# Hybrid attention, convolution and state-space layer: attention of all head pairs as one pipeline of block steps, decay matrices prepared in pairs

## The chip, the cores and the metric

The kernel runs on one core of a Trainium2 chip. The metric is device microseconds of one launch. A core has engines with instruction streams of their own: TensorE (PE in the profile; its weight loads are PEld), VectorE (DVE), ScalarE (ACT), GpSimd (POOL) and SyncE (SP), which here issues most of the loads. They meet only through semaphores. TensorE's matmuls and transposes write into PSUM; ACT and DVE empty it. Each engine takes its instructions strictly in the order in which they stand in its stream.

## The reference

One layer of a hybrid backbone over 128 context tokens and 256 latent tokens (384 together), model width 2048. Cut to what matters here:

```python
hcur = x * (1 + sc1) + sh1                     # modulation 1
q, k, v, u, gt, z, xbc, dt = split(hcur @ w_in)
o_a = attention(q, k, v)                       # 16 heads of 64: context rows dense,
                                               # latent rows over a window plus cached context keys
o_b = silu(layer_norm(dwconv31(u * sigmoid(gt))))
y   = ssd_scan(x, dt, a, B, C, h0)             # both directions, chunks of 128 tokens
      # decay matrix seg = exp(cs_i - cs_j); scores = (C B^T) * seg; y_diag = scores @ (x dt)
o_c = rms_norm((y_f + y_b + d_skip * xs) * silu(z))
mix = concat(o_a, o_b, o_c) @ w_out
x   = layer_norm(ALPHA * x + g1 * mix)
hcur = x * (1 + sc2) + sh2                     # modulation 2
x   = layer_norm(ALPHA * x + g2 * conv_ffn(hcur))
```

All of it is float32 with outputs for both token groups, the context keys and values, and the final states.

## The kernel before

The 384 tokens are three blocks of 128: block 0 is the context, blocks 1 and 2 the latents. A product with a large weight is taken as three fp32r matmuls: weight and activation are split into a high part (a cast on ACT, `whi`, `hl`) and a remainder (a subtraction on DVE, `wlo`, `hl`), and high by high, high by low and low by high are summed in PSUM. These triples (lines 454 to 456 and 460 to 462) are called the main matmuls here.

Up to 275 us the kernel takes modulation 1 and the first part of the input projection; from 590 us on the rest of the output projection, a layer norm and the feed-forward part. The change lies in the stretch between, 275 to 590 us. There a main stream runs: the projections for z and dt, for v, then eight pairs of key and query tiles (one per pair of heads), then the first column group of the output projection (`wo_group(0)`), whose sixteen row blocks come in `ORDER`: the convolution's four (8 to 11), attention 0 to 3, the state space's four (12 to 15), attention 4 to 7. `cat_split` casts and subtracts a row block before it is used. The order of PE's instructions in this stretch is exactly the order in which the program issues them; the other engines' streams are arranged by a scheduler from priorities.

Between the main matmuls stand steps of side work, which are Python generators. The class `_Flow` keeps a clock of assumed PE time: each `flow.tick(us)` of the main stream moves it on, and generators whose due time has come run one step. A step ends with `yield cost, delay`: its assumed PE time and how long until its next step is due. The generators are `tok_gen` (transposes of the state-space inputs), `ssm_gen` (which calls `chunk_steps` for each of three chunks of tokens and adds "ssm" to the set `ready` at its end), `conv_ln_gen` (the layer norm of the convolution), `attn_gen`, `mod2_gen` (part of modulation 2 on PE, lines 768 to 801, whose raw weights lie in the three `v` buffers) and `sh2_gen`, which begins when "ssm" is ready and sums one shift of modulation 2 on DVE (line 832).

- `attn_gen` handles one head pair: `scores` of block 0; then three times `turned` of a block (six transposes of the probabilities into PSUM tiles `at`, copied out by ACT, lines 723 and 725) with `scores` of the next block behind it (lines 695 to 713: PE, then a maximum on DVE, exponential on ACT, reciprocal on DVE, scaling on ACT into `p`, three buffers); then `values` (line 736, into one more `at` tile, copied out by ACT at line 739). There are two `at` tiles in all. From head pair 5 on, a pair begins only when "ssm" is ready.
- `chunk_steps` makes for each of two head groups the decay matrix W (`decays`: DMA and mask on POOL, exponentials on ACT, products on DVE), waits 15 us of flow time, and multiplies (lines 576 to 582).
- `conv_ln_gen` normalises four channel blocks in place in `cvo` and ends with SiLU (line 397) into four new `t` buffers, which become row blocks 8 to 11.
- `mod2_end` adds the bias and either writes the gate by four small DMAs on POOL's queue (group 0) or transposes the scales (group 1). Its two work tiles are `gb` buffers, of which there are three, which also carry the attention's bias tables.

Of the kernel before, what the change touches and what calls it, by code (L numbers as in the profile page):

```python
# [99 lines left out]
def _build(tc, ctx, a):  # L100
# [39 lines left out]
    def gb_t():  # L140
        return sbt([128, 640], "gb", 3)
# [223 lines left out]
    def conv_ln_gen():  # L365
        while flow.bg:
            yield 0.0, 1.0
        yield 0.0, 3.0
        n = 399
        ps = at_t()  # L370
        for i in range(4):
            PE.matmul(ps[:, :n], ones, cvo[i][:, :n], start=i == 0, stop=i == 3)
        mu = g_t()
        S.activation(out=mu[:, :n], in_=ps[:, :n], func=AF.Copy, scale=1.0 / 512)
        yield 2.7, 3.0
        sqs = []
        for i in range(4):
            V.tensor_tensor(out=cvo[i][:, :n], in0=cvo[i][:, :n], in1=mu[:, :n], op=ALU.subtract)
            sq = g_t()
            S.activation(out=sq[:, :n], in_=cvo[i][:, :n], func=AF.Square)  # L380
            sqs.append(sq)
            yield 0.0, 2.0
        sm = at_t()
        for i in range(4):
            PE.matmul(sm[:, :n], ones, sqs[i][:, :n], start=i == 0, stop=i == 3)
        rs = g_t()
        S.activation(out=rs[:, :n], in_=sm[:, :n], func=AF.Sqrt, scale=1.0 / 512, bias=eps_t)
        yield 2.7, 0.0
        for c0, c1 in ((0, 133), (133, 266), (266, 399)):
            yield 0.0, 3.0  # L390
            V.reciprocal(out=rs[:, c0:c1], in_=rs[:, c0:c1])
        for i in range(4):
            yield 0.0, 2.0
            V.tensor_tensor(out=cvo[i][:, :n], in0=cvo[i][:, :n], in1=rs[:, :n], op=ALU.mult)
        for i in range(4):
            c = t_t(T)
            for (c0, c1, o0) in ((0, PT, 0), (PT, T, 143)):
                S.activation(out=c[:, c0:c1], in_=cvo[i][:, o0:o0 + c1 - c0], func=AF.Silu,
                             scale=P_("cln_g", i), bias=P_("cln_b", i))
            cat[8 + i] = c  # L400
            ready.add(8 + i)

    xact = [None] * 8
    xtok = [None] * 3
# [164 lines left out]
    def chunk_steps(c):  # L569
        y = m_t()  # L570
        V.tensor_tensor(out=hv(y), in0=hv(xtok[c]), in1=bc(P_("d_skip", 0, 8), 2, 64), op=ALU.mult)
        for g in range(2):
            W = decays(c, g)
            yield 0.0, 15.0
            psg = at_t()
            PE.matmul(psg[:, :128], xact[4 + g][:, OFF[c]:OFF[c] + 128], xact[6 + g][:, OFF[c]:OFF[c] + 128])
            V.tensor_tensor(out=W, in0=W, in1=bc(psg[:, :128], 1, 4), op=ALU.mult)
# [163 lines left out]
    qk = {}  # L741

    def attn_gen():
        for hp in range(8):
            while hp not in qk or (hp >= 5 and "ssm" not in ready):
                yield 0.0, 0.5
            q, k = qk[hp]
            bias = [gb_t() for _ in range(2)]
            for e in range(2):
                G.dma_start(out=bias[e], in_=a["bias"][2 * hp + e])  # L750
            p = scores(hp, q, k, 0, bias)
            yield 0.65, 5.5
            pts = []
            for blk in range(3):
                pts.append(turned(blk, p))
                if blk < 2:
                    p = scores(hp, q, k, blk + 1, bias)
                yield (1.25, 1.8, 0.75)[blk], (6.0, 6.0, 2.5)[blk]
            values(hp, pts)
            ready.add(hp)  # L760
            yield 2.0, 0.0

    gS = {}

# [16 lines left out]

    def mod2_end(g):
        ps = gS.pop(g)
        sm = gb_t()[:, :512]
        if g == 0:
            bg = gb_t()[:, :512]
            pinned(bg, a["bgate"])
            with tc.high_priority(offset=HP):
                V.tensor_tensor(out=sm, in0=ps, in1=bg, op=ALU.add)
# [175 lines left out]
    def cat_split(k):  # L965
# [6 lines left out]
        ta, tb = cg0[k // 4]  # L972
        ch[k], cl[k] = ta[:, k % 4, :], tb[:, k % 4, :]
        with tc.high_priority(offset=HP):
            split(cat[k], ch[k], cl[k])

    cg0 = [None] * 4
    with tc.manual_schedule(engines={mybir.EngineType.PE}):
# [360 lines left out]
```

## Time and profile before

| quantity | value |
|---|---|
| median of three runs | 1825.29 us (1822.78 to 1829.71) |
| the profiled execution's own time | 1823.79 us |
| its span, first to last instruction | 1822.0 us |
| mean granted TensorE clock | 0.995 |
| PE busy | 1784.0 us (98%) |
| DVE busy | 1216.2 us (67%) |
| ACT busy | 780.6 us (43%) |
| POOL busy | 64.2 us (4%) |

The 1.8 us between span and time lie outside the first and last instruction. A timeline row gives the start of an instruction, its duration and, in brackets, the time its engine was idle before it and what ended that. Matmuls overlap, so what one costs the stream is read from the distance between starts: the main matmuls stand 0.23 us apart and last 0.39 us each.

### The profile page before, as it was taken

How to read it: one execution, taken by the hardware profiler on the slowest of the kernel's cores; microseconds unless marked ns; L12 is line 12 of the kernel's file. 1: busy time of each engine (PE TensorE's matmuls, PEld its weight loads, DVE VectorE, ACT ScalarE, POOL GpSimd, SP SyncE). 2: the span in 40 equal slices, each digit the busy share in tenths (PEclk: the TensorE clock that was granted, in tenths of full speed). 3: DMA queues.
4: the chain of work that ended last, by engine and by line, in shares of the span. 5: the costliest groups of instructions: out<-in, count | busy, mean ns of one | idle time of the engine just before them, and what ended most of it. 6: DMA issues, size and time to landing. Idle time of an engine off the chain costs nothing. (4 is left out here: it accounts for less than half of the span.)

```text
span 1822.0 us, 28856 instructions
## 1 busy us (share of the span) xinstructions
PE 1784.0 (98%) x10794; PEld 1621.9 (89%) x10794; DVE 1216.2 (67%) x2587; ACT 780.6 (43%) x1467; POOL 64.2 (4%) x149
## 2 busy tenths in 40 slices
PE   7999999989998999999999999999999999999998
PEld 6888997878886899999989999988999988999987
DVE  3866899775599977667534676545666544766577
ACT  4223454556664336444333444323444423444424
POOL 0000001011002000000000000000000000000000
PEclk9999999999998999999999999999999999999999
DMA  8899467656798852444544454444544444445454
GB/s 314 312 317 323 142 202 253 234 191 217 242 337 303 268 176 64 147 141 145 155 125 137 162 174 145 150 127 133 174 159 152 151 124 143 158 149 157 122 150 139
DMA packets 113260, 337.76 MB, mean 185 GB/s; under 512 B 13096, under 2 KB 17672, under 8 KB 113120
## 3 DMA queue, kind: packets, MB, share of 16 engines
q1 hardware_dynamic: 105888, 311.65, 52.2%
q0 software_dynamic: 7232, 24.28, 4.3%
q8 instruction: 84, 1.38, 0.3%
q14 instruction: 56, 0.46, 0.1%
HBM read 331.08 MB, written 4.79 MB: 184 GB/s over the span
## 5 line engine op out<-in xcount | busy, mean ns | idle before, releaser
L229 ACT CAST whi<-raw 128x512 fp32r<-128x512 f32 (+1 forms) x755 | 467.8, 621 | 878.0 <-PE mm L461 289.5
L230 DVE TENSOR_TENSOR wlo<-raw,whi 128x512 fp32r<-128x512 f32 (+1 forms) x755 | 519.1, 689 | 409.9 <-ACT whi L229 405.0
L460 PE MATMUL mm<-hl,whi 128*128 128x384 f32 x1245 | 426.4, 342 | 1.5 <-ACT whi L229 1.2
L461 PE MATMUL mm<-hl,whi 128*128 128x384 f32 x1245 | 419.9, 337 | 0.0
L462 PE MATMUL mm<-hl,wlo 128*128 128x384 f32 x1245 | 419.2, 337 | 0.0
L460 PEld LDWEIGHTS mm<-hl,whi 128*128 128x128 f32 x1245 | 233.8, 188 | 11.7 <-issue 4.9
L461 PEld LDWEIGHTS mm<-hl,whi 128*128 128x128 f32 x1245 | 234.0, 188 | 1.1 <-DVE wlo L230 0.4
L462 PEld LDWEIGHTS mm<-hl,wlo 128*128 128x128 f32 x1245 | 233.9, 188 | 0.0
L460 PE MATMUL sc<-hl,whi 128*128 128x384 f32 x659 | 222.9, 338 | 0.0
L461 PE MATMUL sc<-hl,whi 128*128 128x384 f32 x659 | 221.9, 337 | 0.0
L462 PE MATMUL sc<-hl,wlo 128*128 128x384 f32 x659 | 221.8, 337 | 0.0
L460 PEld LDWEIGHTS sc<-hl,whi 128*128 128x128 f32 x659 | 123.7, 188 | 2.9 <-ACT whi L229 1.4
L461 PEld LDWEIGHTS sc<-hl,whi 128*128 128x128 f32 x659 | 123.7, 188 | 0.1
L462 PEld LDWEIGHTS sc<-hl,wlo 128*128 128x128 f32 x659 | 123.7, 188 | 0.0
L832 DVE SCALAR_TENSOR_TENSOR junk<-raw,gb 128x512 bf16<-128x512 f32 x128 | 87.5, 684 | 50.0 <-DMA raw<-wg 49.9
L454 PE MATMUL mm<-whi,hl 128*128 128x512 f32 (+2 forms) x293 | 101.2, 346 | 1.2 <-ACT hl L245 1.1
L456 PE MATMUL mm<-whi,hl 128*128 128x512 f32 (+2 forms) x293 | 99.5, 340 | 0.0
L455 PE MATMUL mm<-wlo,hl 128*128 128x512 f32 (+2 forms) x293 | 99.3, 339 | 0.0
L456 PE MATMUL mm<-whi,t 128*128 128x512 f32 (+1 forms) x232 | 89.7, 387 | 0.0
L454 PE MATMUL mm<-whi,t 128*128 128x512 f32 (+1 forms) x232 | 89.6, 386 | 0.0
L455 PE MATMUL mm<-wlo,t 128*128 128x512 f32 (+1 forms) x232 | 89.6, 386 | 0.0
L832 DVE SCALAR_TENSOR_TENSOR junk<-m,m 128x512 bf16<-128x512 f32 x128 | 87.9, 687 | 2.1
(353 smaller groups left out, 2486.7 us busy)
## 6 DMA issues: line engine op xcount, KB each, us to landing
raw<-wu SPq DMA_DIRECT2D x176, 512.0 KB, 3.5
raw<-wd SPq DMA_DIRECT2D x79, 512.0 KB, 3.6
m<-wm SPq DMA_DIRECT2D x128, 256.0 KB, 5.5
v<-wm SPq DMA_DIRECT2D x64, 512.0 KB, 5.7
raw<-wA SPq DMA_DIRECT2D x32, 512.0 KB, 5.3
raw<-wqk SPq DMA_DIRECT2D x32, 512.0 KB, 4.2
m<-wsh SPq DMA_DIRECT2D x64, 256.0 KB, 5.7
raw<-wo SPq DMA_DIRECT2D x32, 512.0 KB, 4.9
```

The costliest lines, as they stand in the source:

```text
L229: S.copy(out=hi[:, :w], in_=rw)
L230: V.tensor_tensor(out=lo[:, :w], in0=rw, in1=hi[:, :w].bitcast(F32), op=ALU.subtract)
L454: PE.matmul(ps[:, :n], A, hi[:, w0:w0 + n], start=k == 0, stop=False)
L455: PE.matmul(ps[:, :n], A, lo[:, w0:w0 + n], start=False, stop=False)
L456: PE.matmul(ps[:, :n], B, hi[:, w0:w0 + n], start=False, stop=k == last)
L460: PE.matmul(ps[:, :T], A, hh[k], start=k == k0, stop=False)
L461: PE.matmul(ps[:, :T], A, hl[k], start=False, stop=False)
L462: PE.matmul(ps[:, :T], B, hh[k], start=False, stop=k == k1)
L832: V.scalar_tensor_tensor(out=j, in0=w, scalar=1.0, in1=cbc[s], op0=ALU.mult, op1=ALU.mult, accum_out=macc[:, 16 * s + kt, kq:kq + 1])
```

## The change

It has four parts. `attn_gen` becomes one pipeline over all 24 block steps: a block's transposes stand ahead of the next block's scores also across head pairs, a block step is due 6.5 us after the last (5.0 for the last pair), and a pair's `values` moves into the second block step of the next pair, ahead of that step's transposes. `chunk_steps` makes both decay matrices of a chunk first (delays 9 and 7) and then uses both; its two delays of 15 go. The convolution's SiLU writes in place in `cvo`, in two column segments (`CSEG`), and `cat_split` casts and subtracts from there in two pieces each. `mod2_end` takes one `v` buffer for its two work tiles in place of two `gb` buffers.

```diff
         for i in range(4):
-            c = t_t(T)
-            for (c0, c1, o0) in ((0, PT, 0), (PT, T, 143)):
-                S.activation(out=c[:, c0:c1], in_=cvo[i][:, o0:o0 + c1 - c0], func=AF.Silu,
+            for c0, c1 in CSEG:
+                S.activation(out=cvo[i][:, c0:c1], in_=cvo[i][:, c0:c1], func=AF.Silu,
                              scale=P_("cln_g", i), bias=P_("cln_b", i))
-            cat[8 + i] = c
             ready.add(8 + i)
+
+    CSEG = ((0, PT), (143, 143 + ST))
...
+        Ws = [decays(c, 0)]
+        yield 0.0, 9.0
+        Ws.append(decays(c, 1))
+        yield 0.0, 7.0
         for g in range(2):
-            W = decays(c, g)
-            yield 0.0, 15.0
+            W = Ws[g]
...
     def attn_gen():
+        p, pts, done = None, [], None
         for hp in range(8):
             while hp not in qk or (hp >= 5 and "ssm" not in ready):
                 yield 0.0, 0.5
...
-            p = scores(hp, q, k, 0, bias)
-            yield 0.65, 5.5
-            pts = []
             for blk in range(3):
-                pts.append(turned(blk, p))
-                if blk < 2:
-                    p = scores(hp, q, k, blk + 1, bias)
-                yield (1.25, 1.8, 0.75)[blk], (6.0, 6.0, 2.5)[blk]
-            values(hp, pts)
-            ready.add(hp)
-            yield 2.0, 0.0
+                cost = 0.65 if blk == 0 else 1.1
+                if blk == 1 and hp:
+                    values(hp - 1, done)
+                    ready.add(hp - 1)
+                    cost += 1.7
+                if p:
+                    pts.append(turned((blk - 1) % 3, p))
+                    cost += 0.7
+                if blk == 0:
+                    done, pts = pts, []
+                p = scores(hp, q, k, blk, bias)
+                yield cost, 6.5 if hp < 7 else 5.0
+        pts.append(turned(2, p))
+        yield 0.75, 2.5
+        values(7, pts)
+        ready.add(7)
+        yield 2.0, 0.0
...
     def mod2_end(g):
         ps = gS.pop(g)
-        sm = gb_t()[:, :512]
+        vv = v_t()
+        sm, bg = vv[:, 0, :], vv[:, 1, :]
         if g == 0:
-            bg = gb_t()[:, :512]
...
-            split(cat[k], ch[k], cl[k])
+            if 8 <= k < 12:
+                for (s0, s1), (c0, c1) in zip(CSEG, ((0, PT), (PT, T))):
+                    split(cvo[k - 8][:, s0:s1], ch[k][:, c0:c1], cl[k][:, c0:c1])
+            else:
+                split(cat[k], ch[k], cl[k])
```

PE has the same instructions before and after, in another order. The lines of the attention move down by three in the changed file (723 becomes 726, 698 and 700 become 701 and 703, 736 becomes 739). Three places of PE's stream show what moves.

The first is the last head pair, near the end of the stretch. Before, from the transposes of its block 0 on (two with 128 columns, then three and three):

```order
L723 MATMUL at_6485<-cons_66,p_6435 128x128
L723 MATMUL at_6489<-cons_66,p_6442 128x128
L698 MATMUL sc_6493<-qk_5825,qk_5955 128x256
L698 MATMUL sc_6494<-qk_5825,qk_5955 128x256
L700 MATMUL sc_6493<-ckv_3083,qk_5955 128x128
L700 MATMUL sc_6494<-ckv_3083,qk_5955 128x128
L723 MATMUL at_6525<-cons_66,p_6501 128x128 x3
L723 MATMUL at_6531<-cons_66,p_6508 128x128 x3
L698 MATMUL sc_6537<-qk_5825,qk_5955 128x256
L698 MATMUL sc_6538<-qk_5825,qk_5955 128x256
L700 MATMUL sc_6537<-ckv_3083,qk_5955 128x128
L700 MATMUL sc_6538<-ckv_3083,qk_5955 128x128
```

and now the transposes of the last pair's block 1 with the scores of its block 2, up to the first main matmuls behind them:

```order
L726 MATMUL at_6413<-cons_66,p_6336 128x128 x3
L726 MATMUL at_6419<-cons_66,p_6343 128x128 x3
L701 MATMUL sc_6425<-qk_5936,qk_6121 128x256
L701 MATMUL sc_6426<-qk_5936,qk_6121 128x256
L703 MATMUL sc_6425<-ckv_3083,qk_6121 128x128
L703 MATMUL sc_6426<-ckv_3083,qk_6121 128x128
L454 MATMUL mm_6123<-whi_6457,hl_6154 128x512
L455 MATMUL mm_6123<-wlo_6458,hl_6154 128x512
L456 MATMUL mm_6123<-whi_6457,hl_6155 128x512
L454 MATMUL mm_6124<-whi_6457,hl_6154 128x512
```

Before, twelve rows of transposes and scores stand together. Now nine triples of main matmuls (`mm`) stand between those scores and the next transposes.

The second is the hand-over between two head pairs. Before, the last values of head pair 5 (`at_6079`) stand ahead of the block 0 scores of pair 6, and the main stream follows:

```order
L736 MATMUL at_6079<-pt_6028,vt_327 64x128
L736 MATMUL at_6079<-pt_6034,vt_327 64x128
L736 MATMUL at_6079<-pt_6028,vt_328 64x128
L736 MATMUL at_6079<-pt_6034,vt_328 64x128
L695 MATMUL sc_6106<-qk_5597,qk_5696 128x128
L695 MATMUL sc_6107<-qk_5597,qk_5696 128x128
L454 MATMUL mm_5957<-whi_6066,hl_5960 128x512
L455 MATMUL mm_5957<-wlo_6067,hl_5960 128x512
L456 MATMUL mm_5957<-whi_6066,hl_5961 128x512
```

and now the same place for a pair's last values (`at_5962`), in the second block step of the next pair:

```order
L739 MATMUL at_5962<-pt_5861,vt_328 64x128
L739 MATMUL at_5962<-pt_5867,vt_328 64x128
L726 MATMUL at_5979<-cons_66,p_5875 128x128
L726 MATMUL at_5983<-cons_66,p_5882 128x128
L701 MATMUL sc_5987<-qk_5616,qk_5795 128x256
L701 MATMUL sc_5988<-qk_5616,qk_5795 128x256
L703 MATMUL sc_5987<-ckv_3083,qk_5795 128x128
L703 MATMUL sc_5988<-ckv_3083,qk_5795 128x128
L460 MATMUL mm_5939<-hl_82,whi_5946 128x384
```

The values are now followed at once by two transposes into two further `at` tiles, then by scores.

The third is a state-space step, the product of line 541 into an `at` tile that line 549 on DVE reads. Before it had main matmuls behind it, then an attention step:

```order
L541 MATMUL at_4132<-m_4082,btok_3131 128x256 x2
L460 MATMUL mm_4041<-hl_82,whi_4048 128x384
L461 MATMUL mm_4041<-hl_83,whi_4048 128x384
L462 MATMUL mm_4041<-hl_82,wlo_4049 128x384
L460 MATMUL mm_4041<-hl_82,whi_4048 128x384
```

and now the attention's transposes come right behind it:

```order
L786 MATMUL gm_2796<-v_3792,cond_63 32x256 x4
L541 MATMUL at_3951<-m_3901,btok_3131 128x256 x2
L726 MATMUL at_3957<-cons_66,p_3856 128x128 x3
L726 MATMUL at_3963<-cons_66,p_3863 128x128 x3
L701 MATMUL sc_3969<-qk_3621,qk_3734 128x256
L701 MATMUL sc_3970<-qk_3621,qk_3734 128x256
L703 MATMUL sc_3969<-ckv_3083,qk_3734 128x128
```

The main matmuls that stood between the two uses of `at` tiles have gone from this place.

## Rows read from the trace of the kernel before

**Rows 1.** The page's first part, busy time of PE over the whole span; columns are busy us, share of the span, instructions.
```profile
PE 1784.0 (98%) x10794; PEld 1621.9 (89%) x10794; DVE 1216.2 (67%) x2587; ACT 780.6 (43%) x1467; POOL 64.2 (4%) x149
```

**Rows 2.** The timeline of PE around the last head pair, from its last but one block step to the first matmul of the main stream behind it. Columns: start, duration of one group in us, engine, line, operation, tiles, shape, count, and in brackets the idle time before it with what ended it.
```profile
574.08 0.39 PE L700 MATMUL sc<-ckv,qk 64*128 64x128 f32 x4
578.84 1.54 PE L723 MATMUL at<-cons,p 128*128 128x128 f32 x6 [4.37 <-ACT p L713]
...
583.37 0.80 PE L454 MATMUL sc<-whi,hl 128*128 128x512 f32 x1 [1.41 <-ACT p L710]
...
586.95 1.09 PE L723 MATMUL at<-cons,p 128*128 128x128 f32 x6
...
591.15 0.51 PE L454 MATMUL mm<-whi,hl 128*128 128x512 f32 x1 [1.12 <-ACT hl L245]
```

**Rows 3.** The same view some 20 us earlier, at a block step, a values step and the main stream beside them.
```profile
553.77 0.82 PE L723 MATMUL at<-cons,p 128*128 128x128 f32 x6
554.52 0.70 PE L698 MATMUL sc<-qk,qk 64*128 64x256 f32 x4
...
555.37 0.50 PE L454 MATMUL mm<-whi,hl 128*128 128x512 f32 x1
555.71 0.40 PE L455 MATMUL mm<-wlo,hl 128*128 128x512 f32 x1
555.94 0.39 PE L456 MATMUL mm<-whi,hl 128*128 128x512 f32 x1
...
566.83 0.88 PE L736 MATMUL at<-pt,vt 128*64 128x128 f32 x12
...
568.51 0.49 PE L695 MATMUL sc<-qk,qk 64*128 64x128 f32 x4
```

**Rows 4.** The windows view over the stall of rows 2. Columns: stretch, its length, busy us (and instructions) of PE, PEld, DVE, ACT, POOL, the granted TensorE clock, the DMA share and GB/s.
```profile
575.00:580.00 5.00, 1.16 (x6) 1.14 (x6) 4.80 (x18) 2.58 (x7) 0.00 (x0) 0.73 0.62 216
580.00:585.00 5.00, 3.59 (x14) 2.53 (x13) 4.06 (x15) 2.61 (x8) 2.14 (x4) 0.50 0.61 172
585.00:590.00 5.00, 5.00 (x41) 3.90 (x39) 4.46 (x14) 1.34 (x3) 2.03 (x4) 0.75 0.89 223
```

**Rows 5.** The timeline of PE, the nine places between 325 and 573 us where it idled 0.4 us or more.
```profile
344.75 0.55 PE L723 MATMUL at<-cons,p 128*128 128x128 f32 x3 [0.57 <-ACT pt L725]
...
376.07 0.52 PE L723 MATMUL at<-cons,p 128*128 128x128 f32 x3 [1.68 <-DVE m L549]
...
393.81 1.07 PE L581 MATMUL at<-m,m 128*128 128x64 f32 x8 [1.20 <-DVE m L577]
...
408.61 1.50 PE L775 MATMUL gm<-v,cond 128*32 128x256 f32 x24 [1.44 <-DVE gb L789]
...
450.76 0.55 PE L723 MATMUL at<-cons,p 128*128 128x128 f32 x3 [1.48 <-ACT g L387]
...
464.02 0.33 PE L723 MATMUL at<-cons,p 128*128 128x128 f32 x1 [0.45 <-ACT p L713]
...
472.99 0.55 PE L723 MATMUL at<-cons,p 128*128 128x128 f32 x3 [0.47 <-ACT p L713]
...
532.16 0.55 PE L723 MATMUL at<-cons,p 128*128 128x128 f32 x3 [0.69 <-ACT p L713]
...
564.19 0.66 PE L798 MATMUL at<-cons,gb 128*128 128x128 f32 x4 [0.43 <-ACT pt L725]
```

**Rows 6.** The timeline of PE: the values of head pair 4, the last state-space transposes, the first scores of head pair 5.
```profile
486.17 0.61 PE L736 MATMUL at<-pt,vt 128*64 128x128 f32 x8
...
503.74 0.66 PE L605 MATMUL at<-cons,m 128*128 128x128 f32 x4
...
506.43 0.49 PE L695 MATMUL sc<-qk,qk 64*128 64x128 f32 x4
```

**Rows 7.** Two timelines of the values step of head pair 5, first PE's last matmuls of it, then ACT's copy that empties its PSUM tile.
```profile
537.50 0.61 PE L736 MATMUL at<-pt,vt 128*64 128x128 f32 x8
...
538.15 0.48 ACT L739 COPY t<-at 128x384 f32<-128x384 f32 x1 [1.07 <-PE at L736]
```

**Rows 8.** The timeline of DVE at the state-space step of line 549, whose output the transposes at 376.07 us in rows 5 had to wait for.
```profile
375.24 0.68 DVE L549 TENSOR_TENSOR m<-m,at 128x512 f32<-128x512 f32 x1
```

**Rows 9.** The DMA view of 385 to 425 us, its list of issues. Columns: output and input, queue, operation, count, KB each, median us from issue to landing.
```profile
v<-wm SPq DMA_DIRECT2D x7, 512.0 KB, 4.6
...
gd<-gb POOLq DMA_DIRECT2D x4, 4.0 KB, 4.8
```

**Rows 10.** The timeline of ACT, a table load and the two normalised segments of one channel block behind it.
```profile
456.13 1.28 ACT L398 ACT_TABLE_LOAD   x1
457.43 0.99 ACT L398 ACTIVATE t<-t,par 128x128 f32<-128x128 f32 x2
```

**Rows 11.** The windows view again, the columns of rows 4, for three stretches in the middle of the region and for one ahead of the stall.
```profile
400.00:425.00 25.00, 23.32 (x191) 20.20 (x191) 10.33 (x21) 10.68 (x24) 5.76 (x11) 1.00 0.60 201
425.00:450.00 25.00, 24.02 (x147) 19.33 (x147) 14.94 (x33) 22.16 (x58) 3.58 (x7) 1.00 0.65 216
450.00:475.00 25.00, 23.32 (x193) 19.87 (x194) 14.12 (x31) 23.08 (x46) 0.00 (x0) 1.00 0.51 171
513.00:568.50 55.50, 54.38 (x383) 42.81 (x381) 54.13 (x159) 32.18 (x77) 4.81 (x9) 1.00 0.96 342
```

**Rows 12.** The groups of DVE by shape, 300 to 600 us: the row of line 832, the products that sum one shift of the second modulation. Columns: line, engine, operation, tiles, shapes, count, then busy us, mean ns of one, and idle us before.
```profile
L832 DVE SCALAR_TENSOR_TENSOR junk<-m,m 128x512 bf16<-128x512 f32 x88 | 60.4, 686 | 1.4
```

## The prediction

> **What bounds the kernel now.** I read the page's busy times first. PE is busy 1784.0 us of the span of 1822.0 [rows 1], so the kernel is bound by TensorE, and its number of matmuls does not change. What a change of order can give is PE's idle time, the time that it runs at its lower clock, and the little that a switch between kinds of work costs. So I went on to PE's timeline from 275 to 590 us, the only stretch that the change touches, and looked for idle time in brackets. It sits in two kinds of places.
>
> The first is the end of the stretch. The last head pair has no main matmuls left between its block steps. PE waits 4.37 us for the softmax of block 1, then 1.41 and 1.12 us more [rows 2]: 6.90 us idle. The granted clock falls to 0.73, 0.50 and 0.75 of full in three successive windows [rows 4], so between the 2.4 and the 1.2 GHz level, after a window in which PE was busy 1.16 of 5 us. From the end of the last scores before it (574.08 + 0.39 = 574.47) to the next main matmul (591.15) it takes 16.68 us. The same instructions 20 us earlier, at full clock: transposes 554.52 - 553.77 = 0.75, scores 555.37 - 554.52 = 0.85, values 568.51 - 566.83 = 1.68, one main matmul 0.23 [rows 3]. The end holds two sets of transposes, one of scores, one values step and nine main matmuls (eight of them fill 583.37 to 586.95 [rows 2], 0.45 each, twice the 0.23). That is 2 x 0.75 + 0.85 + 1.68 + 9 x 0.23 = 6.1 us. The loss is 16.68 - 6.1 = 10.5 us, 6.9 of it idle, 3.6 the lower clock.
>
> "TensorE: Matmul & The Clock Gate" of the Trainium skill, section "HAM oscillation — how this bites in real kernels", charges half of all throttled time. By rows 4 the slow time would be 5 x (0.54 + 1.0 + 0.5) = 10.2 us, so 5.1 us, and the loss 12.0. I keep the sum from rows, since slow time in which PE is idle costs nothing twice.
>
> The second kind is nine short waits of 0.43 to 1.68 us between 325 and 573 us [rows 5]; their sum is 8.41 us. Three of them are transposes that find `p` unfinished (0.45, 0.47, 0.69), two are transposes that wait for an `at` tile (1.68 behind DVE's line 549, 1.48 behind ACT's line 387 with a table load), one is the gate product that waits for DVE to add the bias (1.44); in the last three PE waits for a copy on ACT or a product on DVE in the same way (0.57, 0.43, 1.20).
>
> **Why the end goes.** The last pair is late because attention stands still: the values of pair 4 are at 486.17 us, and pair 5 begins at 506.43, right behind the last state-space transposes at 503.74 [rows 6]. That is the condition on "ssm", 506.43 - 486.78 = 19.7 us. `chunk_steps` now waits 9 + 7 in place of 15 + 15 units of flow time per chunk, 14 less in each of three chunks. In the changed order of PE the last line 608 stands at row 2185 and the first scores of pair 5 at row 2316, so the condition no longer stops anybody. The attention's 24 steps then lie evenly: each has 18 to 39 main matmuls ahead of its transposes, 4 to 9 us at 0.23, against the 4.37 that a softmax took with PE idle. Behind the last pair's block 1 there are 27 (the first place in the order), and behind its values 18 ahead of the first that needs them. I take all 10.5 us as gained; that some short wait comes back is priced below.
>
> **The change part by part.** Against the profiled execution (1823.79 us, 1822.0 of it span):
> - End stall: -10.5 (bounds -12 to 0, the last if the pairs are late again).
> - The nine waits: all nine places change their neighbours, so all 8.41 go, and new ones are counted below. -8.4.
> - Switches: behind a block the main matmuls start with a distance of 555.71 - 555.37 = 0.34 in place of 0.23 [rows 3], 0.11 each. Side work now comes in 41 runs in place of 50, since transposes, values and scores go together: 9 x 0.11 = -1.0.
> - Values ahead of transposes, seven times: `at` has two tiles. The first transposes take the free one, the second wait for the tile of `values`, that is for ACT's copy. PE ended at 537.50 + 0.61 = 538.11, the copy ran from 538.15 for 0.48 [rows 7], so the tile is free 0.52 us later; a transpose takes 0.75 / 6 = 0.12. 0.4 each, 7 x 0.4 = +2.8. That is the least it can be. Were ACT in the middle of something it is more: with a table load of 1.28 [rows 10] ahead, up to 1.5 each, 10.5. ACT is busy 32.18 of 55.5 us there [rows 11]; I take the lower end all the same, since in rows 7 the copy began 0.04 us after PE's end.
> - One values step falls into the convolution's run of SiLUs on ACT (each two segments 0.99 [rows 10]): +0.7 (0 to 1.5).
> - Line 541 right ahead of transposes (the third place in the order): their second `at` tile waits for DVE's line 549, 0.68 [rows 8], which before with main matmuls between still cost 1.68 in one place [rows 5]: +1.0, and 0.3 for a second place of the kind (0 to 3.4 together).
> - Other short waits of the kinds in rows 5: state-space products back to back 0.7, `p` 1.2 (before 1.61), W unfinished since two are made together 0.6, the scale transposes 0.5. Together +3.0 (0 to 6).
> - `mod2_end` now holds one of three `v` buffers until the gate's four small writes have landed, so one load of the next weights is held. The writes take 4.8 us from issue to landing and the load 4.6 [rows 9]; with the issue of four writes on POOL and the addition, an estimate of 12.5 to 13.6 us, against some 13.5 us of PE's work until the piece that needs it in the changed order. SP stands behind this load with others for the main stream, which are issued several buffers ahead. +0.5 (0 to 4). On the other side the 1.44 behind the bias [rows 5] goes, counted above.
> - DVE: the sum of line 832 begins when "ssm" is ready, so about 25 us earlier, and some 25 more of its 88 products [rows 12] stand ahead of the last scores. In 513 to 568.5 DVE is already busy 54.13 of 55.5 us [rows 11], and PE was idle little. An attention maximum can stand behind one product, 0.69, at a time; with several us of cover I take +1.5 (0 to 17).
> - The convolution's casts and subtractions in two pieces: a few tenths of a us on ACT and DVE, four times, hidden behind PE's main stream; without cover 4 x 0.3. Four `t` buffers fewer: 0, PE waited for none in rows 5.
>
> "DMA: Bandwidth & Descriptors" of the Trainium skill, section "Anatomy of one DMA — SWDGE (gpsimd) path", gives about 2.0 us fixed per DMA of POOL. By it the four writes would land early enough for no wait at all; rows 9 show 4.8 us for 4 KB, which I used.
>
> Sum: -10.5 - 8.4 - 1.0 + 2.8 + 0.7 + 1.3 + 3.0 + 0.5 + 1.5 = -10.1 us. The profiled execution is 1.5 us below the median, so the sum is taken from the median: 1825.3 - 10.1 = 1815.2 us.
>
> **The rivals.**
> - Given back at the hand-over (B). With one cast or SiLU of about 0.6 us on ACT ahead of each copy, each hand-over costs 1.0 in place of 0.4: +4.2, 1819.4 us; with a table load ahead, 1.5: +7.7, 1822.9 us. For it: ACT takes its instructions in order and is busy more than half the time. Against it: rows 7 again.
> - DVE becomes the bound (C, slower). If the 25 us of line 832 that move ahead cannot use idle time of DVE, the last softmax is late by 25 x 0.69 = 17 us, the end stall stays, and the clock falls with it, 3.6 more as in rows 2: 1815.2 + 17 + 3.6 = 1836 us. It decides as soon as more than about 9 of these 25 products (6 us, the mean cover) stand in front of one block step. For it: DVE's 54.13 of 55.5 us. Against it: from 400 to 475 us DVE is busy 10.33 + 14.94 + 14.12 = 39.4 of 75 [rows 11], and the attention that now runs in the pause of rows 6 takes its share out of the crowded end.
> - More is gained (D). If only the hand-overs and the wait at line 549 cost something: -19.9 + 3.8 = -16.1, 1809.2 us. For it: five of the nine waits in rows 5 are under 0.7 us, so little more cover would have hidden them.
> - The change does not do what it says (E). If the condition on "ssm" still stops pair 5, because W is not ready when its products are due, the end stall stays: -10.1 + 10.5, about 1825.7 us. Against it: the order on PE is fixed, and there the pairs stand early; only waits could bring the stall back.
>
> **How the numbers follow.** My forecast gets 0.55, with a range of its own of 1812 to 1818.5 from the small terms. B 0.22, C 0.09, D 0.09, E 0.05. The likeliest gives 1815.2 us. The range reaches down to D, 1809, and up past B's dear end and near E, 1823.5; C and part of E are left out. 0.5% is 9.1 us, about what a measurement here can tell from no change: faster means below 1816.2. Of the forecast's 0.55 about three quarters lie there, 0.41, with D 0.50. The same: 0.14 + 0.22 + 0.05 = 0.41. Slower: C, 0.09.
>
> **What would show it.** PE's timeline near the end of the stretch without an idle time above 1.5 us, and granted clock 1.00 in all its windows; the second column group of the output projection begins about 10 us earlier. At each values step (now line 739) a gap of about 0.4 us in the transposes behind it, ended by ACT's copy: if it is 1 or more, B. At line 726 behind line 541 about 1 us ended by DVE. Line 786 with no wait for line 800. If transposes wait for `p` again and again, each with DVE's line 843 in front of the maximum, C holds and the forecast is wrong; if the waits all fall below 0.3 us, D. A stretch of attention without block steps between 470 and 510 us would say that E holds.

## The result, and the profile after

The changed kernel takes 1811.64 us (median of five runs, 1811.02 to 1812.67) beside 1822.78 us for the kernel before in the same comparison (1820.45 to 1829.71, five runs; the 1825.29 that the prediction started from is the median of the first three of them): a ratio of 0.9934 with the interval 0.9912 to 0.9955, 11.1 us. The forecast was 10.1 us less, 1815.2 us. The two profiled executions stand 1823.79 - 1812.03 = 11.8 us apart, their spans 1822.0 - 1810.2 = 11.8.

The page's busy times of the changed kernel, to be held against [rows 1]:

```profile
PE 1780.8 (98%) x10794; PEld 1620.9 (90%) x10794; DVE 1213.4 (67%) x2591; ACT 774.6 (43%) x1466; POOL 62.6 (3%) x149
```

PE has as many matmuls as before and 3.2 us less busy time, though nothing was taken out: slow matmuls count as longer ones, and before three windows of 5 us at the end lay below the full clock [rows 4]. The windows view of the changed kernel over the same three stretches of time (columns as there):

```profile
575.00:580.00 5.00, 5.00 (x24) 4.17 (x25) 4.93 (x16) 0.85 (x2) 1.03 (x3) 1.00 1.00 342
580.00:585.00 5.00, 5.00 (x23) 3.90 (x22) 5.00 (x10) 1.63 (x3) 1.03 (x2) 1.00 0.90 315
585.00:590.00 5.00, 5.00 (x23) 4.10 (x22) 4.97 (x13) 1.24 (x2) 0.00 (x0) 1.00 0.55 193
```

PE is busy throughout and the granted clock is 1.00 where it was 0.73, 0.50 and 0.75. The timeline of PE in the changed kernel shows the last state-space transposes, the first scores of pair 5 and the last pair's steps (start, duration, engine, line, operation, tiles, shape, count, idle time ahead):

```profile
455.47 0.60 PE L608 MATMUL at<-cons,m 128*128 128x128 f32 x4
...
483.05 0.49 PE L698 MATMUL sc<-qk,qk 64*128 64x128 f32 x4
...
556.34 0.87 PE L726 MATMUL at<-cons,p 128*128 128x128 f32 x6
557.14 0.70 PE L701 MATMUL sc<-qk,qk 64*128 64x256 f32 x4
...
564.38 0.82 PE L726 MATMUL at<-cons,p 128*128 128x128 f32 x6
...
569.26 0.88 PE L739 MATMUL at<-pt,vt 128*64 128x128 f32 x12
```

Pair 5 starts at 483.05 us, where it was 506.43 [rows 6], and 27.6 us behind the last state-space transposes, where it was 2.7, so the condition no longer holds it. The last two sets of transposes carry no bracket: their `p` is there when PE comes, the 4.37 us of [rows 2] are gone. These are all waits of 0.2 us or more that PE now has between 325 and 600 us, in the place of [rows 5] and of the three in [rows 2]:

```profile
338.42 0.33 PE L726 MATMUL at<-cons,p 128*128 128x128 f32 x1 [0.89 <-ACT p L716]
349.61 0.52 PE L726 MATMUL at<-cons,p 128*128 128x128 f32 x3 [1.36 <-DVE m L549]
369.25 0.33 PE L726 MATMUL at<-cons,p 128*128 128x128 f32 x1 [0.32 <-ACT t L742]
400.91 0.33 PE L726 MATMUL at<-cons,p 128*128 128x128 f32 x1 [0.32 <-ACT t L742]
429.38 0.33 PE L726 MATMUL at<-cons,p 128*128 128x128 f32 x1 [0.46 <-ACT t L742]
438.16 0.52 PE L726 MATMUL at<-cons,p 128*128 128x128 f32 x3 [0.43 <-DVE m L595]
464.77 0.33 PE L726 MATMUL at<-cons,p 128*128 128x128 f32 x1 [1.14 <-ACT t L742]
492.81 0.33 PE L726 MATMUL at<-cons,p 128*128 128x128 f32 x1 [0.32 <-ACT t L742]
520.40 0.33 PE L726 MATMUL at<-cons,p 128*128 128x128 f32 x1 [0.99 <-ACT t L742]
538.35 0.55 PE L726 MATMUL at<-cons,p 128*128 128x128 f32 x3 [0.23 <-ACT p L716]
547.34 0.33 PE L726 MATMUL at<-cons,p 128*128 128x128 f32 x1 [0.32 <-ACT t L742]
574.91 0.66 PE L809 MATMUL at<-cons,v 128*128 128x128 f32 x4 [0.61 <-DVE v L805]
```

Their sum is 7.39 us. Before, the nine waits of [rows 5] with the three of [rows 2] make 15.31, and four smaller ones (0.24 to 0.40) 1.15, together 16.46. So 9.1 of the 11.8 us are idle time, and the rest is the clock, the switches between kinds of work, and 0.4 us that the executions differ by before the change begins (the gate product of line 775, now 786, starts at 271.68 us before and at 271.30 now). Seven rows end with ACT's line 742: the hand-over between pairs, in which the second transposes wait for the copy of the values. Two of the seven are dear, and ACT's timeline of the changed kernel says why:

```profile
462.49 1.86 ACT L397 ACTIVATE t<-t,par 128x256 f32<-128x256 f32 x4
464.26 0.46 ACT L742 COPY t<-at 128x384 f32<-128x384 f32 x1
...
518.65 1.32 ACT L245 CAST hl<-t 128x256 fp32r<-128x256 f32 x4
519.88 0.47 ACT L742 COPY t<-at 128x384 f32<-128x384 f32 x1
```

The copy stands right behind the convolution's SiLUs in the one case, and behind the casts of its four row blocks, now in pieces, in the other.

### The profile page after: what moved, and what is told of

The parts are those of the page before. It is cut to its first block, busy times and chain, and to the rows that moved or that the text cites. A ratio compares the mean times of both kernels' runs of the same rounds, so it can differ in the third digit from the quotient of the medians.

```text
span 1810.2 us, 28844 instructions
## 1 busy us (share of the span) xinstructions
PE 1780.8 (98%) x10794; PEld 1620.9 (90%) x10794; DVE 1213.4 (67%) x2591; ACT 774.6 (43%) x1466; POOL 62.6 (3%) x149
```

## The experiments

One table first, since four runs are read by it. Idle time is the sum of PE's waits of 0.2 us or more in its timeline, in the middle (300 to 566 us) and at the end (566 to 600); the clock is the lowest of the windows of 5 us from 300 to 600.

| kernel | idle, middle | idle, end | lowest clock | median us |
|---|---|---|---|---|
| before | 9.56 | 6.90 | 0.50 (end) | 1822.78 to 1825.83 |
| changed | 6.78 | 0.61 | 1.00 | 1811.64 |
| e1, decay matrices and mod2_end | 9.50 | 3.01 | 0.50 (middle) | 1818.21 |
| e2, attention alone | 8.42 | 3.27 | 0.66 (middle) | 1823.80 |
| e3, changed with delays 15 and 15 | 14.01 | 3.69 | 0.53 (middle) | 1825.12 |
| e4, before without the condition | 11.51 | 0.50 | 0.50 (middle) | 1817.84 |

The median of before is given as the lowest and highest of its medians over the comparisons. They lie 3 us apart, so each run's ratio is taken to the kernel before in its own comparison.

**Decay matrices and mod2_end, without the new attention.**

```diff
     def chunk_steps(c):
...
+        Ws = [decays(c, 0)]
+        yield 0.0, 9.0
+        Ws.append(decays(c, 1))
+        yield 0.0, 7.0
         for g in range(2):
-            W = decays(c, g)
-            yield 0.0, 15.0
+            W = Ws[g]
...
     def mod2_end(g):
         ps = gS.pop(g)
-        sm = gb_t()[:, :512]
+        vv = v_t()
+        sm, bg = vv[:, 0, :], vv[:, 1, :]
         if g == 0:
-            bg = gb_t()[:, :512]
```

> The kernel before with the pairwise decay matrices (delays 9 and 7) and mod2_end in a v buffer; the attention stays as before. Theory (the late state space held up pair 5, and that alone made the stall at the end): pair 5 is no longer held, a pause without attention between 487 and 506 us is gone. On PE the last pair has 27 main matmuls ahead of block 1's transposes and 8 ahead of block 2's, so the 4.37 us of idle time fall to about 4.37 - 8 x 0.23 = 2.5, with 0.5 ahead of the values and 1.1 behind them: 4 to 5.5 us lost at the end in place of 10.5, the wait of 1.44 gone, the other short waits much as before. 5 to 7 us below before, about 1816. Rival (the pipeline of 24 even steps takes the stall away, the state space's time does not matter): 9 us or more still lost at the end, 1820 or above.

Measured: 1818.21 us, ratio 0.9967 (0.9956 to 0.9979), 6.1 us below before. At the end 1.60, 1.12 and 0.29 us of idle time are left, and the clock is 1.00 there. That is the theory, with somewhat less left than its 4 to 5.5 us; the rival asked for 9 us or more. The total lies in the theory's 5 to 7 us too, but in part by luck, for the middle is not "much as before". A wait of 4.88 us, with the clock at 0.50 behind it, takes back part of what the end gave:

```profile
361.39 2.07 PE L541 MATMUL at<-m,btok 128*128 128x256 f32 x4 [4.88 <-ACT pt L728]
```

**The new attention alone.**

```diff
     def attn_gen():
+        p, pts, done = None, [], None
         for hp in range(8):
...
             for blk in range(3):
...
+                if blk == 1 and hp:
+                    values(hp - 1, done)
...
```

The whole of the new `attn_gen` is in the change's diff.

> The kernel before with the new attn_gen alone; the decay matrices keep their delays of 15 and 15. Theory: pair 5 is still held until the state space ends, so the last pair is late: on PE 9 main matmuls and a small step stand ahead of block 1's transposes, 8 and a small step ahead of block 2's, and 1 ahead of the values. Idle there about 2.2 + 2.2 + 0.5 + 1.1 = 6 us, some of it at the lower clock, 6 to 8 us lost at the end; at the hand-overs seven waits of 0.4 or more. 3 to 7 us below before, about 1818. Rival (the pipeline alone takes the stall away): under 2 us lost at the end, 1814 or below.

Measured: 1823.80 us, ratio 0.9997 (0.9987 to 1.0006). The theory asked for 6 to 8 us lost at the end and for 3 to 7 us less than before, and is wrong in both. At the end 3.27 us are idle in place of 6.9, at full clock, though pair 5 is still held (its first scores are at 503.43 us), so the even steps alone take about two thirds of the 10.5 us there. But nothing of it is left in the total: the middle has waits of 2.40 us (at 369.82, a hand-over), 1.65 and 1.73 us, and the clock falls to 0.66 behind the first and to 0.74 behind the third.

**The changed kernel with late decay matrices.**

```diff
         Ws = [decays(c, 0)]
-        yield 0.0, 9.0
+        yield 0.0, 15.0
         Ws.append(decays(c, 1))
-        yield 0.0, 7.0
+        yield 0.0, 15.0
```

> The changed kernel with the two delays of the decay matrices set to 15 and 15 (9 and 7 in it). Theory: the condition on the state space holds pair 5 again; the order at the end is that of the run with the new attention alone, so 6 to 8 us come back at the end, with windows below a clock of 1.00: 1817 to 1819. Rival (the early state space is worth nothing once the attention is a pipeline): 1813 or below, no wait above 1.5 us at the end.

Measured: 1825.12 us, ratio to before 1.0002 (0.9993 to 1.0011), where the changed kernel has 0.9934: some 12 to 13 us above it. The rival (1813 or below) has fallen: the two delays are worth all that the change gains. But they are not worth it where the theory looked. The end has 3.69 us of idle time and a clock of 1.00; the middle has 14.0, of which one hand-over takes 6.41. The timeline of PE in this run, then that of ACT:

```profile
373.16 0.47 PE L726 MATMUL at<-cons,p 128*128 128x128 f32 x1 [6.41 <-ACT t L742]
...
363.13 0.62 ACT L229 CAST whi<-raw 128x512 fp32r<-128x512 f32 x1
368.00 1.28 ACT L563 ACTIVATE m<-m,ncs 128x128 f32<-128x128 f32 x4 [4.25 <-POOL m L560]
372.34 0.40 ACT L563 ACTIVATE m<-m,ncs 128x128 f32<-128x128 f32 x1 [3.06 <-POOL m L560]
372.64 0.46 ACT L742 COPY t<-at 128x384 f32<-128x384 f32 x1
```

and of POOL:

```profile
361.37 0.56 POOL L558 DMA_DIRECT2D m<-csd  x1 [1.88 <-PE at L541]
365.30 0.54 POOL L558 DMA_DIRECT2D m<-csd  x1 [3.37 <-DVE m L566]
367.33 0.63 POOL L560 TENSOR_SCALAR_AFFINE_SELECT m<-m 128x512 f32<-128x512 f32 x1 [1.49 <-DMA m<-csd]
371.60 0.70 POOL L560 TENSOR_SCALAR_AFFINE_SELECT m<-m 128x512 f32<-128x512 f32 x1 [3.64 <-DMA m<-csd]
```

In the changed kernel the exponentials of this chunk run from 354 to 358 us, and no hand-over comes until 369. Here, read backwards: the copy of the values (line 742), whose input PE had finished by 366.5 us, stands behind the exponentials of the decay matrices (line 563). These wait for the masks on POOL (line 560), each of them for its DMA, and the DMAs were issued late: the first at 361.37, behind PE's line 541, the second at 365.30, when DVE's line 566 had freed a buffer. ACT is idle 4.25 + 3.06 us with work behind the instruction that waits, and PE stands with it. The Trainium skill, page "TensorE: Matmul & The Clock Gate", section "Architectural detail: the array is 16× 32×32, not 1× 128×128", says that ACT's and DVE's queues are strictly first in, first out. The rows agree, with these 7.31 us.

**Before without the condition on the state space.**

```diff
-            while hp not in qk or (hp >= 5 and "ssm" not in ready):
+            while hp not in qk:
```

> The kernel before without the condition that head pairs 5 to 7 wait for the state space; nothing else. Theory: pair 5 starts at about 487 us in place of 506, on PE 27 main matmuls stand ahead of each of the last pair's transposes and 2 ahead of its values. Idle at the end 0.5 + 1.1, 1.5 to 2.5 us lost in place of 10.5; the nine short waits stay. 7 to 9 us below before, about 1815. Rival (something else makes the last pairs late, the order of DVE's work above all): a wait of 3 us or more stays at the end, 1819 or above.

Measured: 1817.84 us, ratio 0.9965 (0.9952 to 0.9978), 6.4 us below before. Pair 5 starts at 487.34 us, and one wait of 0.50 us is left at the end:

```profile
487.34 0.49 PE L695 MATMUL sc<-qk,qk 64*128 64x128 f32 x4
...
585.91 0.50 PE L456 MATMUL mm<-whi,hl 128*128 128x512 f32 x1 [0.50 <-DVE hl L246]
```

This one line takes the whole end stall away, which is the theory; the rival (something else makes the last pairs late) has fallen. The total is 2 to 3 us short of the theory's 1815, and a new wait of 2.86 us has come in the middle:

```profile
535.25 0.80 PE L454 MATMUL mm<-whi,hl 128*128 128x512 f32 x1 [2.86 <-ACT qk L677]
```

and the windows view of this run on either side of it:

```profile
530.00:535.00 5.00, 2.39 (x12) 1.78 (x10) 5.00 (x11) 5.00 (x14) 0.00 (x0) 0.95 0.90 306
535.00:540.00 5.00, 4.75 (x28) 2.27 (x29) 5.00 (x15) 3.61 (x10) 0.00 (x0) 0.50 0.96 311
```

ACT (the fourth pair of numbers) is busy all 5 us ahead of it, most of them with the casts of row blocks for the output projection (line 245), ahead of the copy that PE needs.

**Values behind the transposes and scores.** Two runs, the second beside the changed kernel itself on one chip.

```diff
-            pts = sbt([128, n], f"pt{n}", 4 if blk else 2)
+            pts = sbt([128, n], f"pt{n}", 4)
...
-                if blk == 1 and hp:
-                    values(hp - 1, done)
-                    ready.add(hp - 1)
-                    cost += 1.7
                 if p:
                     pts.append(turned((blk - 1) % 3, p))
...
                 p = scores(hp, q, k, blk, bias)
+                if blk == 1 and hp:
+                    values(hp - 1, done)
+                    ready.add(hp - 1)
+                    cost += 1.7
```

> The changed kernel with the values of the pair before moved behind the step's transposes and scores, and four buffers in place of two for the transposed block 0, which the values then still read. Theory (the second transposes of a hand-over wait only for ACT's copy of the values' tile): the seven waits that end with that copy (0.32 four times, 0.46, 0.99, 1.14, 3.87 us in all) vanish, nothing takes their place, 1807 to 1808.5. Rival (PE waits for the same copy at its next use of an at tile, or the scores' softmax is late in its turn): 1810.5 to 1812.

> The changed kernel unaltered, on the same chip as the next run, so that the two can be held against each other. Theory: 1811 to 1813, and the small waits at 350 us and at the hand-overs the same as in the first profile to some tenths. Rival (the waits change from execution to execution by more than the values' place is worth): sums of idle time that differ by 2 us or more between two profiles of this kernel.

> The run with the values last, again, beside the changed kernel on one chip. Theory (the seven waits for the values' copy, 3.87 us, go and 1 to 2 us of other waits come): 1.5 to 3 us below the changed kernel. Rival (no gain once both run on one chip): within 1 us of it.

Measured: 1809.60 us (ratio to before 0.9917, 0.9903 to 0.9931, and again 0.9917 in the second comparison), between the first theory's 1807 to 1808.5 and its rival's 1810.5 to 1812. On one chip it is 1810.53 (1809.47 to 1811.41) beside 1811.08 (1810.21 to 1814.59) for the changed kernel. The seven waits for line 742 are gone, as the theory says, but others have come: 1.64 us in which the values wait for ACT's line 728 (at 517 us), the scale transposes' 0.61 is 1.27, and some of about half a microsecond. So half a microsecond of gain is left, less than these runs can tell from none: the rival of the last run. The second profile of the changed kernel also shows how firm single waits are. The sums are 7.39 and 6.75 us, so its rival, 2 us or more of difference, has fallen. But the transposes behind line 541 wait 1.36 for DVE's line 549 in the first and 0.56 for ACT's line 728 in the second, where a wait of 0.79 for a `qk` tile follows at 358 us; the hand-over behind the SiLUs is 1.14 and 0.53; and the other six hand-overs are equal to the hundredth.

**Late decay matrices and values last.** The edits of the run with late decay matrices and of the run with the values last, together.

> The run with the late decay matrices (15 and 15), with the values moved behind the transposes and scores as in the run before. Theory (the loss in the middle of that run is one hand-over copy that stands on ACT behind exponentials of line 563, which wait for POOL's mask and its DMA): the wait of 6.41 us at the hand-over goes, the fall of the clock behind it goes, and so do six waits of 0.32; 1825 becomes 1813 to 1816, with 3 to 4 us at the end left. Rival (PE stands for W itself, or for the next tile that the copy blocks): a wait of 4 us or more stays between 360 and 380 us, 1821 or above.

Measured: 1823.94 us, ratio 0.9992 (0.9983 to 1.0001). The wait of 6.41 has become one of 2.99, and the clock stays at 1.00 behind it, but the blocked copy is not the only one. The timelines of PE and ACT in this run at the same place:

```profile
369.02 0.88 PE L739 MATMUL at<-pt,vt 128*64 128x128 f32 x12 [2.99 <-ACT pt L728]
...
368.12 0.69 ACT L563 ACTIVATE m<-m,ncs 128x128 f32<-128x128 f32 x2 [4.24 <-POOL m L560]
368.72 0.41 ACT L728 COPY pt<-at 128x128 f32<-128x128 f32 x2
```

The copies of the transposes (line 728) stand behind the same exponentials, and the values wait for them. So the place on ACT is confirmed and the cure was none: whatever of the attention's needs ACT there is late. Later 2.05 and 1.20 us (for `p`, with the clock at 0.66 behind them) and 3.72 us (the cast of a pair's values, at 576 us, with the clock at 0.54 around it) come on top. The theory's number, 1813 to 1816, is wrong. The rival's, 1821 or above, is right, but not by the wait of 4 us or more that it asked for between 360 and 380 us.

**The convolution's output in buffers of its own again.**

```diff
         for i in range(4):
-            for c0, c1 in CSEG:
-                S.activation(out=cvo[i][:, c0:c1], in_=cvo[i][:, c0:c1], func=AF.Silu,
+            c = t_t(T)
+            for (c0, c1, o0) in ((0, PT, 0), (PT, T, 143)):
+                S.activation(out=c[:, c0:c1], in_=cvo[i][:, o0:o0 + c1 - c0], func=AF.Silu,
...
+            cat[8 + i] = c
...
-            if 8 <= k < 12:
...
+            split(cat[k], ch[k], cl[k])
```

> The changed kernel with the convolution's SiLU going into four buffers of its own again, cast and subtracted in one piece each. Theory (hidden beside the main stream, the prediction's 0): within 1 us of the changed kernel, 1810.5 to 1812.5, and the hand-over at 520 us, whose copy stood behind four casts of 256 columns, changes by some tenths. Rival (keeping the output in place is what frees buffers and removes waits): 1814 or above, with new waits that end at a t buffer.

Measured: 1811.25 us (ratio 0.9927, 0.9913 to 0.9941): the theory. The hand-over at 520 us falls from 0.99 to 0.62, and none of the waits that are new (0.40 for a `qk` tile, 0.76 for `p`) is for a `t` buffer of the convolution. This part of the change gives nothing here.

**More work on DVE.**

```diff
             dve_gemv(w, kt, kq)
+            j = sbt([128, 512], "junk", 1, mybir.dt.bfloat16)
+            V.scalar_tensor_tensor(out=j, in0=w, scalar=1.0, in1=cbc[0], op0=ALU.mult, op1=ALU.mult,
+                                   accum_out=macc[:, kt, kq:kq + 1])
```

> The changed kernel with one product more on DVE at each step of the sum of line 843 (the same product once more into the same place, the output is unchanged): three in place of two per step, some 44 more of 0.69 + 0.08 us between 440 and 580 us, 34 us. DVE is idle there about 0.5 us of 25. Theory (DVE is at its limit there and PE is spared only because what DVE does late is not yet waited for): the remainders wlo and the softmax come late, PE waits for DVE again and again, 10 to 34 us slower, 1822 to 1845. Rival (the products can pile up behind the rest at no cost to PE): below 1815.

Measured: 1821.44 us, 9.8 above the changed kernel, so near the theory's lower end, but for another reason. Up to the scale transposes PE is not late by anything: they stand at 573.91 us in this run and at 574.91 in the changed kernel. What is late is DVE's work, and it shows 100 us later. The windows view of the changed kernel behind the stretch and at the layer norm:

```profile
600.00:625.00 25.00, 25.00 (x109) 20.27 (x108) 13.61 (x21) 7.45 (x12) 1.07 (x2) 1.00 0.52 148
625.00:650.00 25.00, 25.00 (x125) 20.96 (x124) 11.13 (x19) 8.78 (x16) 1.07 (x2) 1.00 0.46 132
...
675.00:700.00 25.00, 23.18 (x190) 22.06 (x190) 20.00 (x43) 20.38 (x52) 0.54 (x1) 1.00 0.05 12
```

the same of this run:

```profile
600.00:625.00 25.00, 25.00 (x110) 20.25 (x109) 24.66 (x60) 7.43 (x13) 1.08 (x2) 1.00 0.72 233
625.00:650.00 25.00, 25.00 (x129) 21.14 (x128) 24.62 (x62) 8.73 (x17) 1.08 (x2) 1.00 0.52 164
...
675.00:700.00 25.00, 17.57 (x110) 15.54 (x109) 20.27 (x54) 15.44 (x39) 0.54 (x1) 0.80 0.03 11
```

and its timeline of PE in the layer norm, where the waits end at DVE:

```profile
677.43 0.63 PE L1055 MATMUL at<-cons,vt 128*128 128x128 f32 x4 [1.73 <-DVE vt L1050]
...
688.28 2.14 PE L1055 MATMUL at<-cons,vt 128*128 128x128 f32 x8 [3.53 <-DVE vt L1050]
```

DVE (the third pair of numbers) fills 24.6 of 25 us in this run where it had 13.6 and 11.1: the products give way to the rest and run on into the output projection (56 of them start behind 600 us, none in the changed kernel), until the layer norm needs what they hold up. There the waits of PE are 5.6 us longer together, and the clock is 0.80 in place of 1.00 in those 25 us.

**mod2_end alone.** The part of the first run's diff that concerns `mod2_end`, and nothing else.

> The kernel before with mod2_end in a v buffer alone. Theory (the 1.44 us that the gate product waited for DVE's addition came from the gb buffers; the v buffer costs nothing since its next load lands in time): that wait goes, no wait for v comes, the end stall stays as it was: 1 to 2 us below before, within what can be measured. Rival (the held v buffer delays a load): a new wait of 1 us or more at line 778 ended by the load of v, no gain.

Measured: 1823.76 us, ratio 0.9994 (0.9984 to 1.0003). The wait of 1.44 is gone and none for a `v` buffer has come, as the theory says; its 1 to 2 us can't be told from nothing here. In this profile the clock fell to 0.66 behind the wait at line 581. From that wait (393.81 us before, 394.08 here) to the transposes of line 723 behind it (397.42 and 399.23) that cost 1.5 us, all that the 1.44 gave.

**All that looked useful, together.** Values last, the convolution's own buffers, and

```diff
         V.tensor_copy(out=sm, in_=ps)
-        yield 0.0, 2.0
+        yield 0.0, 6.0
```

> The changed kernel with the values last (four buffers for the transposed block 0), the convolution's output in four buffers of its own as before, and a delay of 6 in place of 2 ahead of the scale transposes. Theory (the waits left in the run with the values last, 1.64 at 517 us behind ACT's casts and 1.27 at the scale transposes, come from the four pieces of 256 columns and from DVE's copy being due too soon): both fall below 0.6, 1807 to 1809. Rival (they move to the next step): as the run with the values last, 1809 to 1810.5.

Measured: 1810.68 us, ratio 0.9925 (0.9912 to 0.9937). The wait of the scale transposes is gone. That of the values at 517 us is 1.27 in place of 1.64, so the casts in pieces were not its main cause, and one of 1.66 us for `p` has come at 536. The rival, with its 1809 to 1810.5, is the closer one. No version beats the changed kernel by more than these comparisons can tell.

## Why the prediction was right

- **The time.** 1811.64 us lies 3.6 us below the forecast 1815.2 and just below the forecast's own 1812 to 1818.5. Of these 3.6, 2.5 us are the median of before, 1825.29 in three runs and 1822.78 in five; the sum itself, -10.1, is 1.0 us short.
- **The end stall, -10.5.** Right in place and size: 0.61 us of idle time, clock 1.00. The cause named, the condition on the state space, is shown by the run without it (0.50 us left). It was not the only way out: with the condition still holding pair 5, the even steps alone bring the end to 3.27 us at full clock. The prediction had put the whole stall on the condition, and the expectations of the runs with the attention alone and with late matrices failed at the end for that.
- **The nine waits, -8.4, and new ones.** They have gone, and new ones came at the places named. Line 541 ahead of transposes: forecast 1.3, measured 1.36 in one profile, and 0.56 behind ACT's line 728 in the other. The other short waits: forecast 3.0, measured 0.89 + 0.43 + 0.23 + 0.61 = 2.2, and 2.9 in the other profile. The `v` buffer: forecast 0.5, no wait; its 12.5 to 13.6 us against 13.5 was close all the same, for in two of the runs with the values last PE waits 0.21 and 0.47 us for the load. DVE: forecast 1.5, nothing on PE that could be put down to it, since the waits of 0.23 and 0.61 us stay at 0.23 and 0.58 with half as many products again.
- **The hand-overs, +2.8, and the SiLUs, +0.7.** Forecast 3.5, measured 3.87: four of 0.32, one of 0.46, 1.14 behind the SiLUs, and 0.99 behind the convolution's casts, which I had entered as hidden. The run with buffers of their own puts 0.37 of these 0.99 down to the pieces, and no time could be told from it.
- **Clock and switches.** Counted 3.6 + 1.0; of the 11.8 us only some 2.3 are neither idle time nor the difference ahead of the change. This term was 2.3 too large, the new waits (7.4 us measured, against 9.8) 2.4, and the two errors cancel: that much of the agreement is luck. Which of the two parts, clock or switches, was too large no run shows. The four waits under 0.4 us, 1.15 together, had no term; they are about what the sum is short of the 11.4 us between the two profiles (11.8 less the 0.4).
- **The rivals.** B had the right place and, in this order of the program, too high a price. But its upper end, 1.5 us for one hand-over, was far too low as a bound: with late decay matrices one takes 6.41 us. The prediction had bounded ACT's delay by what ACT executes, not by what it may stand waiting for. C had the wrong place: DVE's surplus is paid at the layer norm, not in the attention, and the products that moved forward cost nothing that the waits show. There were more of them than the prediction's 25: it read the 88 of [rows 12] as all, but there are 128, of which 40 start behind 600 us before and none now. D was not reached, and E did not happen.
- **Why all of it together.** Each half alone removes most of the end stall and then loses in the middle: 6.1 us gained with the decay matrices, nothing measurable with the attention, 11.1 with both. The prediction added up the changed order alone and had no term for such a loss. That the changed order meets no such loss, while the same order of steps with 14 units of delay more loses the whole gain by waits of 6.41 us and less, it gave no reason for, and in this it was lucky too.

Left open: why a late stretch of decay work meets a hand-over at 365 to 373 us in some orders and not in others was read off the timelines, not varied by itself. The decay matrices were run only together with `mod2_end`; since `mod2_end` alone gives nothing that can be measured, the 6.1 us are put down to them, but by that argument and not by a run.

## What to carry to other kernels

Before a step that needs a small copy on another engine at once, look at what stands ahead of that copy in the engine's order, and bound the wait by what those instructions wait for, through POOL and a DMA if need be, not by how long they run. A stall at the end of a phase can have its cause much earlier (here 70 to 90 us), in a condition that holds one stream back; the gap in that stream's own timeline shows it. And where DVE is full, follow the work that gives way to the rest to where it is needed at last: here the price was paid there.

## What was unexpected of the hardware

The length of PE's idle time did not tell whether the clock falls. Behind 2.86 us without the condition it was 0.50. Behind 2.99 us, the wait at 369 us with late matrices and values last, it stayed at 1.00:

```profile
365.00:370.00 5.00, 2.01 (x28) 1.67 (x28) 1.29 (x4) 1.60 (x6) 1.17 (x2) 1.00 0.97 381
370.00:375.00 5.00, 5.00 (x38) 4.72 (x34) 1.68 (x6) 2.60 (x9) 0.63 (x1) 1.00 0.25 102
```

Behind the wait at line 581, 1.20 us in the kernel before and 1.21 with `mod2_end` alone, the windows view shows for before

```profile
395.00:400.00 5.00, 5.00 (x33) 4.63 (x32) 3.11 (x9) 2.90 (x11) 0.00 (x0) 1.00 0.48 166
```

and for `mod2_end` alone

```profile
395.00:400.00 5.00, 5.00 (x23) 4.78 (x24) 2.28 (x7) 2.38 (x8) 2.04 (x4) 0.66 0.46 166
```

with 23 matmuls in place of 33 in the same 5 us. The same wait, in front of the same matmuls, so cost its own length in one execution and 1.5 us more in the other. They are executions of two kernels; whether two executions of one kernel can differ like this, no run here shows.
